# Ordering 24 in-projection matmuls behind the last filter's norm matmul, and giving the last job's rows of x buffers of their own

## The chip, the core and the metric

The kernel runs on one core of a Trainium2 chip. The metric is the device time of one execution in microseconds (us). TensorE (PE in the profile, with PEld for its weight loads) does the matrix products, VectorE (DVE) the elementwise work on two inputs, ScalarE (ACT) activations, casts and copies out of PSUM, GpSimd (POOL) some subtractions and some DMA issues, SyncE (SP) most DMA issues. Each engine works through its own instructions in the order in which the program lists them for that engine, and waits on semaphores for the others.

## The reference

An encoder layer is applied to two inputs of 1024 rows by 1024 channels, x_prompt (called x0 in the kernel) and x_sample (x1). Cut to what matters:

```python
p = rmsnorm(x, g_pre) @ w_in            # 8 sections of 1024 columns
fv, fg, hv, hg, mg = split(p)           # hv has 3 sections: v, x1, x2
y_f = (fft2_real(fv) * silu(fg)) @ w_fourier_out
v, x1, x2 = split(short_conv(hv, w_short))
z = v
for n, gate in enumerate((x1, x2)):
    z = gate * long_conv(z, kf[n], d[n])      # via FFT, with implicit filters
y_h = (z * silu(hg)) @ w_hyena_out
g_f, g_h = split(sigmoid(mg + b_merge))
return x + rmsnorm((g_f * y_f + g_h * y_h) @ w_out, g_post)
```

The filters `kf` (two orders n, 1024 channels) come from a small network, are multiplied by a decay, divided by the sum of their absolute values over all taps, and transformed. The last line adds the untouched rows of x to the normed output: those rows are the second thing that the change is about.

## The kernel before, in words

All large products are done in a split format: a number is stored as a high and a low part (`wh`, `wl`, `yh`, `yl` and so on), and each product is three matmuls (`mm3`, L469): high by high, high by low, low by high. So one in-projection tile (`inproj`, L838; 128 output channels by 1024 positions, PSUM tile `pin`) is 2 halves q of the contraction, by 2 halves n of the positions, by 4 blocks, by 3, that is 48 matmuls of 128x512, 24 for each q. The first q uses the first four blocks of x, the second q the other four. Two `pin` tiles fit in PSUM at once (`self.psum("mm", 2, "pin", L)`, L841). The weights of each q are loaded (`wr`), rounded on ACT (`wh`, L170) and the remainder is made on POOL (`wl`, L180), with three buffers for each.

The work goes through three phases. `phase_fourier` (L601) does the Fourier branch of both inputs. `phase_main` (L986) first makes the 16 filters in a loop over i (two orders n by eight channel tiles ct), then runs `branches` (L1039). `phase_tail` (L1169) does the remaining gates and the output products.

In the filter loop each filter has two parts. `filter_taps` (L736) makes the taps `T` and the sum of their absolute values in `acc`; its norm is two small products on PE into the tile `pn` (L765 and L766, recorded as two matmuls each), from which DVE makes the reciprocal `invn` (L767) and the skip term `db` (L768, L769). `filter_spectrum` (L773) forms even and odd parts on DVE (`fE`, `fO`, `xp`, `xm`), calls `butterfly` (L658: DVE and ACT make the pieces `b`, `bs`, `bh`, `bl`), then transforms each of four groups with `forward` (L704, tile `pXf`, L788) and turns the results on ACT (`ktmp`, L794, L803, L804) and DVE (`kt`). Between filters the loop runs gate tiles (`spill_gate`, L876), so that PE has in-projections to do. The loop is one filter ahead with its taps: the taps of the last filter are made before the spectrum of the last but one.

`branches` runs the steps of the long convolutions. Ahead of its loop stand `front(0)` (L1053: the in-projection and short convolution of the tile `v`, L1055, then transposes) and `gates(0)` (L1058: the in-projection of the first gate tile, here called x, by `conv(2, 0, ...)`). `conv` (L866) empties a `pin` tile with one activation on ACT (L871) and two operations on DVE (L872 and L873, recorded at L176), after which the PSUM is free. The output of `v` lies in a buffer tagged "u" that it shares with `xm` of the filter spectrum (L781, L869; one buffer); the output of x lies in a buffer tagged "x" (four buffers, shared with the taps). Step 1 then begins with another `v`, which needs a free `pin` tile.

What sets the order: the program is written for a tile framework that fixes each engine's order when the kernel is built. It steps through a simulated timeline and, whenever an engine is free in it, takes among the instructions whose inputs are there the one that stands first in the program. So a later in-projection slides in wherever PE would wait in that simulated timeline, ahead of instructions that stand before it in the program. `tc.issue_after(ins)` adds an order: what is traced in its block on the engine of `ins` is placed behind `ins`. No semaphore and no data dependence comes with it. On the chip each engine keeps the order that was fixed.

The end of the tail: the output product runs as eight jobs (`rows`, L1176), each two blocks of 128 rows. A job's first products are started one job ahead by `first` (L1245), which multiplies by the weight blocks `B11` and `B21`. `B11` lies in the cells x10 to x13 of the pool `xp` (L1431: `("B11", "x1{}", 60)`), and the eighth job's `first` is its last reader. `open_rows` (L1461) loads the job's rows of x (tile `xr`) on SP's queue into the cells st0 and st1 of the pool `gw`, one buffer each, so the load of one job follows the last read of the job before it. `half_row` (L1474) combines the products, `finish` (L1494) and, in the last job, `begin_norm` and `end_norm` (L1504, L1511) make the norm, and `close` (L1488) does `o = half * rs + x` (L1491, recorded at L176) and stores the result (tile `y`, L1492).

Of the kernel before, what the change touches and what calls it, by code (L numbers as in the profile page):

```python
# [16 lines left out]
P = 128  # L17
# [143 lines left out]
class K:  # L161
    def __init__(self, tc, a, dbg=None):
        self.tc, self.nc, self.a = tc, tc.nc, a
        self.dbg = dbg or {}


    def split(self, h, l, src, eng="pool", heng="act"):
# [568 lines left out]
    def filter_taps(self, n, ct, rates, ws):  # L736
        nc, a = self.nc, self.a
        w3, dec = rates
        w3s = ws.tile([P, 4, 256], F32R, tag="t1", name="w3s", bufs=1)
        w3h, w3l = w3s[:, 0], w3s[:, 1]  # L740
        self.split(w3h, w3l, w3, "dve", "act")
        T = [ws.tile([P, 2, 2, 2, P], F32, tag="x", name=f"T{i}", bufs=4) for i in range(2)]
        acc = ws.tile([P, 2, 2, P], F32, tag="yl", name="acc", bufs=2)
        accf = acc.rearrange("p a d c -> p (a d c)")
        for m in range(4):
            ps = self.psum("T", 2, "pft")
            ex = ws.tile([P, 512], F32, tag="yh", name="ex", bufs=2)
            for i in range(2):
                q = 2 * m + i
                s = slice(256 * i, 256 * i + 256)  # L750
                self.mm(ps[:, s], self.hid[:, q * P:(q + 1) * P], w3h, True, False)
                self.mm(ps[:, s], self.hid[:, q * P:(q + 1) * P], w3l, False, True)
                nc.scalar.activation(ex[:, s], dec, AF.Exp, scale=self.vec[:, q:q + 1])
            Tm = T[m // 2][:, m % 2].rearrange("p a d c -> p (a d c)")
            self.mul("dve", Tm, ps, ex)
            nc.scalar.activation(ex if m else accf, Tm, AF.Abs)
            if m:
                self.add("dve", accf, accf, ex)
        db = ws.tile([P, P], F32, tag="db", name="db", bufs=1)
        nc.sync.dma_start(db, a["hyena_d"][n, ct].partition_broadcast(P))  # L760
        self.add("dve", acc[:, 0], acc[:, 0], acc[:, 1])
        self.add("dve", acc[:, 0, 0], acc[:, 0, 0], acc[:, 0, 1])
        sm = acc[:, 0, 0]
        pn = self.psum("T", 2, "pn")
        nc.tensor.matmul(pn[:, 0:P], self.ones[:, 0:1].to_broadcast([P, P]), sm, start=True, stop=True)  # L765
        nc.tensor.matmul(pn[:, P:P + 2], sm, self.ones[:, 0:2], start=True, stop=True)  # L766
        nc.vector.reciprocal(self.invn[:, n * 8 + ct:n * 8 + ct + 1], pn[:, P:P + 1])  # L767
        self.mul("dve", db, pn[:, 0:P], db)  # L768
        self.stt("dve", T[0][:, 0, 1, 0], db, self.vec[:, 9:10], T[0][:, 0, 1, 0])  # L769
        nc.vector.tensor_scalar(T[1][:, 1, 0, 1], T[1][:, 1, 0, 1], self.vec[:, 8:9], None, op0=MUL)  # L770
        return T
# [66 lines left out]
    def inproj(self, sec, mt, b=None):  # L838

        nc, a = self.nc, self.a  # L840
        ps = self.psum("mm", 2, "pin", L)  # L841
        for q in range(2):
            s = slice(512 * q, 512 * q + 512)
            h = self.wp.tile([P, 4, P], F32R, tag="wh", name="wh", bufs=3)
            l = self.wp.tile([P, 4, P], F32R, tag="wl", name="wl", bufs=3)
            parts = [t.rearrange("p a b -> p (a b)") for t in (h, l)]
            kept = self.d_w[sec - 1][mt] if b is not None else None
            if b:
                for t, k in zip(parts, kept):
                    nc.sync.dma_start(t.bitcast(F32), k[:, s])  # L850
            else:
                r = self.wp.tile([P, 512], F32, tag="w", name="wr", bufs=2)
                nc.sync.dma_start(r, a["w_in"][sec, mt][:, s])
                self.split(*parts, r, "pool", "act")
                self.pooled = self.left
                if kept:
                    for t, k in zip(parts, kept):
                        nc.gpsimd.dma_start(k[:, s], t.bitcast(F32))
            for n in range(2):
                for kk in range(4):  # L860
                    k = 4 * q + kk
                    s = slice(512 * n, 512 * n + 512)
                    self.mm3(ps[:, s], (h[:, kk], l[:, kk]), self.X[k][n], k == 0, k == 7)
        return ps

    def conv(self, sec, ct, ws, name, b):  # L866
# [172 lines left out]
    def branches(self, nb, nct, ws, mi):  # L1039

        tc, nc = self.tc, self.nc
        steps = []
        for b in range(nb):
            steps.append((b, 0, 0))
            for c in range(1, nct):
                steps += [(b, 0, c), (b, 1, c - 1)]
            steps.append((b, 1, nct - 1))
        plain = list(self.PLAIN)  # L1050
        Z, X, G = {}, {}, {}

        def front(i):  # L1053
            b, n, c = steps[i]
            src = self.conv(1, c, ws, "v", b) if n == 0 else Z.pop(c)  # L1055
            return self.conv_front(src, ws)

        def gates(i):  # L1058
            b, n, c = steps[i]
            x = self.conv(2 + n, c, ws, f"x{n + 1}", b)  # L1060
            if n and b == 0:
                early = c < NH
                ps = None if early else self.inproj(4, c)
                sg = [self.wp.tile([P, 512], F32, tag="gt", name="sg", bufs=3) for q in range(2)]
                for q in range(2):
                    s = slice(512 * q, 512 * q + 512)
                    if early:
                        nc.sync.dma_start(sg[q], self.d_g[0][4][c][:, s])
                    else:
                        nc.scalar.activation(sg[q], ps[:, s], AF.Silu)  # L1070
                G[i] = sg, early
            X[i] = x

        def close(i):

            if i in G:
                sg, early = G.pop(i)
                for q in range(2):
                    s = slice(512 * q, 512 * q + 512)
                    if early:  # L1080
                        with tc.issue_after(self.rounded.ins):
                            nc.scalar.activation(sg[q], sg[q], AF.Silu)
                    self.mul("dve", X[i][:, s], X[i][:, s], sg[q])
        B = front(0)
        gates(0)
        for i, (b, n, c) in enumerate(steps):
            nxt = None
            if i + 1 < len(steps):
                nxt = front(i + 1)
                gates(i + 1)  # L1090
                if i + 2 < len(steps) and steps[i + 2][0] != steps[i + 1][0]:
                    self.load_x(steps[i + 2][0])
            y = self.conv_back(n, c, B, ws)
            close(i + 1)
            B = nxt
            for _ in range({4: 1, 3: 1, 2: 2, 1: 2}.get(len(steps) - i, 0)):
                self.spill_gate(b, *plain.pop(), ws)
            z = self.gate(n, c, y, X.pop(i))
            if self.due:
                mark = mi.tile([P, 1], F32R, tag="mark", name="mark", bufs=1)  # L1100
                with tc.issue_after(nc.gpsimd.tensor_copy(mark, z[:, 0:1]).ins):  # L1101
                    self.due.pop(0)()
            if n == 0:
                Z[c] = z
                continue
            nc.sync.dma_start(self.d_sh[b][c], z)
            if b == 0 and NF <= c:
                self.spill_gate(0, 0, c, ws)
        with tc.issue_after(self.ended.ins):
            for sec, c in plain:  # L1110
                self.spill_gate(1, sec, c, ws)
# [57 lines left out]
    def phase_tail(self):  # L1169
# [10 lines left out]
        with ExitStack() as es:  # L1180
# [277 lines left out]

            row = {}

            def open_rows(job):  # L1461
                u, t = job
                b, half = u // 2, u % 2
                where = [512 * half + P * (t + j) for j in range(2)]
                x, o = [], []
                for j in range(2):
                    x.append(flat(cell(gw, f"st{j}", "xr")))
                    nc.sync.dma_start(x[j], a[f"x{b}"][where[j]:where[j] + P, :])
                    o.append(flat(cell(xp, f"x0{4 + 2 * (t // 2) + j}", "o")))
                ss = op.tile([P, 2, 2], F32, tag="ss", name="ss", bufs=2)  # L1470
                row.update(b=b, at=where, x=x, o=o, ss=ss)
                return dict(row)
# [132 lines left out]
            Y["T4"] = quad(Z["T4"])  # L1605
            for i, job in enumerate(rows):
                final = i + 1 == len(rows)
                cur = open_rows(job)
                out = lambda job, j, n, p, q, op2: half_row(j, n, p, q, op2)
                pc, u = list(part2(out, job, A, Y, pa, pb, m1))[-1]  # L1610
                if i + 2 == len(rows):
# [105 lines left out]
```

## Time and profile before

| | us |
|---|---|
| median of three timed runs | 2370.41 (2368.41 to 2370.42) |
| the profiled execution, its own time | 2372.98 |
| span of its trace | 2371.2 |
| around the span | 1.78 |

The shares of the span by engine, with the work of the whole program: TensorE is busy for 2321.9 us of it, VectorE for 1970.2, ScalarE for 1118.7, GpSimd for 446.3. The mean clock that the throttle granted to TensorE is 0.996.

How to read it: a line of the timeline gives the start, the length, the engine, the line of the kernel, the operation, output and inputs and the number of instructions; where the engine stood idle before, the idle time and what ended it stand in square brackets. L193, L180, L176 and L170 are helpers that record most operations, so those go by the names of their tiles. A line of the table by windows gives, for a stretch of the trace, its length and the busy time of PE, PEld, DVE, ACT and POOL with the number of instructions, then the granted clock of TensorE, the mean share of the DMA engines and GB/s. Starts of instructions are used below for lengths of streams of matmuls, since these overlap.

### The profile page before, as it was taken

To read this page: it belongs to the slowest core of one execution; us is meant where nothing else is said; L and a number is where in the kernel's file an instruction comes from. 1 tells how busy PE (TensorE), PEld (TensorE's weight loads), DVE (VectorE), ACT (ScalarE), POOL (GpSimd) and SP (SyncE) were. 2 spreads that over 40 slices of the span, in tenths; PEclk is the share of its full clock that TensorE was granted. 3 is DMA by queue.
4 is the path that set the end of the run, shared out by engine and by line. 5 is a ranking of instruction groups with operands and counts; after the bars stand their busy time and mean duration, and the time that the engine had idled before them with its cause. 6 is when DMAs were issued, how large, how long until landed. Compare 5 with 4: busy or idle time off the path is not lost.

```text
span 2371.2 us, 36206 instructions
## 1 busy us (share of the span) xinstructions
PE 2321.9 (98%) x12784; PEld 2016.9 (85%) x12784; DVE 1970.2 (83%) x3438; ACT 1118.7 (47%) x2080; POOL 446.3 (19%) x428
## 2 busy tenths in 40 slices
PE   6999999999999999999999999999999999999998
PEld 5999888888878888888888888888888888888787
DVE  7775788887889999999889998997755578777987
ACT  6654676777653333334223232333443364566443
POOL 3342221222233342322000000122000000101311
PEclk9999999999999999999999999999999999999999
DMA  7636765555566666677464564445954678998654
GB/s 257 219 137 218 270 217 168 176 167 169 189 211 196 208 197 206 201 202 248 156 207 139 178 188 163 151 156 181 340 168 142 217 268 267 265 315 248 187 161 142
DMA packets 246207, 479.69 MB, mean 202 GB/s; under 512 B 24582, under 2 KB 82280, under 8 KB 245706
## 3 DMA queue, kind: packets, MB, share of 16 engines
q1 hardware_dynamic: 222013, 402.25, 51.0%
q0 software_dynamic: 23792, 75.11, 11.2%
q8 instruction: 100, 1.64, 0.3%
q14 instruction: 81, 0.66, 0.1%
q10 hardware_dynamic: 221, 0.04, 0.0%
HBM read 326.82 MB, written 177.73 MB: 213 GB/s over the span
## 4 chain that ended last, share of the span: by engine, by line
PE 54%; DVE 4%; issue 2%; DMA 1%; POOL 0%; ACT 0%; DVEq 0%; SPq 0%; POOLq 0%; ACTq 0%
PE pin L193 18%; PE pg L193 14%; PE pn L193 10%; PE pT L193 5%; PE pX L193 5%; PE tph L904 1%; DVE x L176 0%; DMA k<-d_k 0%; DMA d_m<-gt 0%; DVE t L180 0%; POOL d_m L1358 0%; DVE b L180 0%; DMA wl<-d_s 0%; DVE y L180 0%; DMA xr<-in_x 0%
## 5 line engine op out<-in xcount | busy, mean ns | idle before, releaser
L193 PE MATMUL pin<-x,wh 128*128 128x512 f32 x2816 | 889.7, 391 | 0.0
L193 PEld LDWEIGHTS pin<-x,wh 128*128 128x128 f32 x2816 | 524.4, 188 | 99.3
L193 PE MATMUL pin<-x,wl 128*128 128x512 f32 x1408 | 552.0, 392 | 0.0
L180 POOL TENSOR_TENSOR wl<-wr,wh 128x512 fp32r<-128x512 f32 x128 | 221.8, 1733 | 684.2 <-ACT wh L170 641.0
L193 PEld LDWEIGHTS pin<-x,wl 128*128 128x128 f32 x1408 | 265.2, 188 | 48.5
L193 PE MATMUL pn<-room,wh 128*128 128x512 f32 x864 | 266.4, 389 | 0.6 <-DVE gt L180 0.6
L193 PEld LDWEIGHTS pn<-room,wh 128*128 128x128 f32 x864 | 162.0, 188 | 35.0 <-issue 1.0
L193 PE MATMUL pn<-room,wl 128*128 128x512 f32 x432 | 168.4, 390 | 1.1 <-DVE wl L180 1.1
L180 DVE TENSOR_TENSOR t<-pX,k 128x1024 f32<-128x1024 f32 x128 | 155.7, 1217 | 9.0 <-PE pX L193 4.3
L193 PE MATMUL pX<-bh,cfwd 128*128 128x256 f32 x768 | 162.4, 288 | 0.0
L193 PE MATMUL pT<-cinv,yh 128*128 128x256 f32 x768 | 146.1, 285 | 3.6 <-DVE T0s L180 3.6
L170 ACT CAST wh<-wr 128x512 fp32r<-128x512 f32 x128 | 79.2, 619 | 135.5 <-PE pin L193 102.1
L170 ACT CAST bh<-b 128x512 fp32r<-128x512 f32 x144 | 88.5, 619 | 114.0 <-DVE b L180 82.2
L193 PEld LDWEIGHTS pT<-cinv,yh 128*128 128x128 f32 x768 | 123.0, 191 | 10.7 <-ACT T1s L957 2.7
L193 PEld LDWEIGHTS pX<-bh,cfwd 128*128 128x128 f32 x768 | 127.1, 190 | 2.8 <-issue 0.4
L1358 POOL DMA_DIRECT2D d_m<-gt x32 | 27.1, 848 | 534.0 <-DVE gt L180 497.8
L170 ACT CAST yh<-y 128x512 fp32r<-128x512 f32 x96 | 59.6, 620 | 124.2 <-DVE y L180 123.7
L193 PE MATMUL pT<-cinv,yl 128*128 128x256 f32 x384 | 109.3, 285 | 0.2 <-DVE yl L180 0.2
L193 PE MATMUL pX<-bl,cfwd 128*128 128x256 f32 x384 | 109.2, 284 | 0.0
L180 DVE TENSOR_TENSOR bl<-b,bh 128x512 fp32r<-128x512 f32 x144 | 102.3, 715 | 3.0 <-ACT bh L170 2.7
L1101 POOL CAST mark<-x 128x1 fp32r<-128x1 f32 x30 | 22.4, 746 | 412.3 <-DVE x L176 412.2
L180 DVE TENSOR_TENSOR y<-t 128x512 f32<-128x512 f32 x128 | 91.9, 718 | 6.5 <-PE pT L193 6.2
(362 smaller groups left out, 5174.0 us busy)
## 6 DMA issues: line engine op xcount, KB each, us to landing
k<-d_k SPq DMA_DIRECT2D x128, 512.0 KB, 4.3
wr<-in_w_in SPq DMA_DIRECT2D x128, 256.0 KB, 3.3
d_g<-gt SPq DMA_DIRECT2D x124, 256.0 KB, 3.0
wl<-d_s SPq DMA_DIRECT2D x56, 512.0 KB, 5.7
d_k<-kt SPq DMA_DIRECT2D x128, 128.0 KB, 2.4
d_k<-kt SPq DMA_DIRECT2D x64, 256.0 KB, 3.0
g<-d_g SPq DMA_DIRECT2D x64, 256.0 KB, 5.4
r<-d_g SPq DMA_DIRECT2D x60, 256.0 KB, 5.8
```

Of the source, the lines that this page charges most:

```text
L170: self.rounded = nc.scalar.copy(h, src)
L180: return e.tensor_tensor(out, a, b, op=op)
L193: return self.nc.tensor.matmul(out, lhsT, rhs, start=start, stop=stop, skip_group_check=shared)
L904: nc.tensor.transpose(tp[:, q * P:(q + 1) * P], eo[:, e, q], self.ident)
L1101: with tc.issue_after(nc.gpsimd.tensor_copy(mark, z[:, 0:1]).ins):
L1358: nc.gpsimd.dma_start(dst, t, accum_op=ADD)
```

## The change

It has two parts that share no code. The first: the norm matmul of L766 is remembered in `self.normed` (after the filter loop it is that of the last filter). While `gates(0)` is traced, `self.behind` holds it, and `inproj` puts the 24 matmuls of q = 1 into a block `issue_after`. The 24 of q = 0, the loads and the rounding of the weights, and all other calls of `inproj` are left as they are. The second: the last job of the output product loads its rows of x into the cells x10 and x11 of the pool `xp` instead of st0 and st1.

```diff
@@ filter_taps
-        nc.tensor.matmul(pn[:, P:P + 2], sm, self.ones[:, 0:2], start=True, stop=True)
+        self.normed = nc.tensor.matmul(pn[:, P:P + 2], sm, self.ones[:, 0:2], start=True, stop=True)
@@ inproj
-            for n in range(2):
-                for kk in range(4):
-                    k = 4 * q + kk
-                    s = slice(512 * n, 512 * n + 512)
-                    self.mm3(ps[:, s], (h[:, kk], l[:, kk]), self.X[k][n], k == 0, k == 7)
+            with self.tc.issue_after(self.behind.ins) if q and self.behind else ExitStack():
+                for n in range(2):
+                    for kk in range(4):
+                        k = 4 * q + kk
+                        s = slice(512 * n, 512 * n + 512)
+                        self.mm3(ps[:, s], (h[:, kk], l[:, kk]), self.X[k][n], k == 0, k == 7)
@@ branches
         B = front(0)
+        self.behind = self.normed
         gates(0)
+        self.behind = None
@@ open_rows
-            def open_rows(job):
+            def open_rows(job, own=False):
...
-                    x.append(flat(cell(gw, f"st{j}", "xr")))
+                    x.append(flat(cell(xp, f"x1{j}", "xr") if own else cell(gw, f"st{j}", "xr")))
@@ the loop over the jobs
-                cur = open_rows(job)
+                cur = open_rows(job, final)
```

`self.behind` is set to `None` in the constructor.

More of the change, by code (lines that the diff above doesn't have):

```diff
@@ L1084, in branches @@
         B = front(0)
+        self.behind = self.normed
         gates(0)
+        self.behind = None
         for i, (b, n, c) in enumerate(steps):
```

## The prediction

> **What bounds the kernel now.** I read the page first (who is busy, what ended last), then the chain of waits near the end, then what PE waits for, then the timeline at the two places that the change touches.
>
> ```profile
> PE 2321.9 (98%) x12784; PEld 2016.9 (85%) x12784; DVE 1970.2 (83%) x3438; ACT 1118.7 (47%) x2080; POOL 446.3 (19%) x428
> ...
> PE 54%; DVE 4%; issue 2%; DMA 1%; POOL 0%; ACT 0%; DVEq 0%; SPq 0%; POOLq 0%; ACTq 0%
> ```
>
> PE is hardly ever without work, and PE makes most of the chain that ended last. With the matmuls left as they are, time can only come from places where PE stands still, and from the tail behind its last matmul. The table by windows shows the one large hole of the main phase:
>
> ```profile
> 640.00:667.00 27.00, 27.00 (x151) 23.60 (x150) 24.01 (x58) 18.73 (x41) 10.17 (x12) 1.00 0.74 250
> 667.00:676.90 9.90, 9.90 (x57) 8.39 (x55) 6.67 (x18) 3.40 (x8) 2.33 (x3) 1.00 0.59 186
> 676.90:682.40 5.50, 0.00 (x0) 0.03 (x1) 5.50 (x14) 3.64 (x8) 2.69 (x3) 0.95 0.66 213
> 682.40:686.20 3.80, 3.80 (x21) 3.80 (x22) 3.80 (x8) 1.97 (x4) 0.00 (x0) 0.63 0.49 176
> ```
>
> PE does nothing for 5.50 us while DVE is busy for all of them, and the clock then stands at 0.63 for 3.80 us, which costs 3.80 x 0.37 = 1.4 us more. The timeline says who waits for whom:
>
> ```profile
> 671.12 0.38 PE L765 MATMUL pn<-acc,ones 128*128 128x128 f32 x2
> ...
> 671.48 0.48 PE L193 MATMUL pin<-x,wl 128*128 128x512 f32 x1
> 671.79 0.28 PE L193 MATMUL pXf<-bh,cfwd 128*128 128x256 f32 x1
> ...
> 674.67 0.63 PE L193 MATMUL pin<-x,wh 128*128 128x512 f32 x2
> ...
> 676.51 0.39 PE L193 MATMUL pin<-x,wl 128*128 128x512 f32 x1
> 682.40 1.19 PE L193 MATMUL pXf<-b,cfw 128*128 128x128 f32 x4 [5.50 <-DVE b L180]
> ...
> 686.12 0.63 PE L193 MATMUL pin<-x,wh 128*128 128x512 f32 x2
> ```
>
> The last filter's norm (pn, 671.12) is followed by the rest of the first gate tile's in-projection, and then by nothing until the butterfly of that filter gives b. The other end of that chain is on DVE:
>
> ```profile
> 666.43 0.28 DVE L180 TENSOR_TENSOR acc<-acc 128x128 f32<-128x128 f32 x1
> ...
> 669.14 0.61 DVE L176 SCALAR_TENSOR_TENSOR kt<-pXf,th,ktmp 128x128 f32<-128x128 f32 x2 [1.25 <-ACT ktmp L804]
> 671.65 0.17 DVE L767 RECIPROCAL invn<-pn 128x1 f32<-128x1 f32 x1 [1.91 <-PE pn L766]
> ...
> 680.65 1.27 DVE L176 SCALAR_TENSOR_TENSOR x<-pin,wsh,x 128x1023 f32<-128x1023 f32 x1
> 681.85 0.74 DVE L180 TENSOR_TENSOR b<-bs 128x256 f32<-128x256 f32 x2
> ...
> 684.46 1.27 DVE L176 SCALAR_TENSOR_TENSOR x<-pin,wsh,x 128x1023 f32<-128x1023 f32 x1
> ```
>
> acc, which pn sums up, is there at 666.43 + 0.28 = 666.71, yet pn runs 4.4 us later, and DVE loses 1.91 us waiting for it. From 671.65 on no line up to b at 681.85 carries a wait. So before b DVE is late because pn is late, and pn is late because in-projection matmuls stand ahead of it on PE.
>
> How many of the held 24 these are, the weights tell. Each half tile takes one of three weight buffers in turn (v's two, x's two, the next v's two), so the second half of the next v is cast when the 24 matmuls of x's first half are over (first line of these ACT rows):
>
> ```profile
> 667.96 0.62 ACT L170 CAST wh<-wr 128x512 fp32r<-128x512 f32 x1
> ...
> 677.60 1.09 ACT L871 ACTIVATE x<-pin,wsh 128x1024 f32<-128x1024 f32 x1
> ...
> 680.84 0.40 ACT L690 ACTIVATE bs<-bs 128x256 f32<-128x256 f32 x1
> ```
>
> From 667.96 to 671.12 are 3.16 us, 14 matmuls at 0.23 us (nine matmuls start from 674.67 to 676.51, eight steps of 0.23), and 10 come behind pn (one at 671.48, nine from 674.67). 14 + 10 are the 24 of q = 1: the count closes.
>
> The other place is the end of the program. Timeline of DVE, SP and ACT there:
>
> ```profile
> 2339.74 0.44 SPq L1468 DMA_DIRECT2D xr<-in_x  x1
> 2355.59 1.07 SPq L1492 DMA_DIRECT2D y<-o  x2
> 2356.76 0.41 SPq L1468 DMA_DIRECT2D xr<-in_x  x1
> ...
> 2358.23 0.43 SPq L1468 DMA_DIRECT2D xr<-in_x  x1
> ```
>
> ```profile
> 2362.50 0.16 DVE L1520 SCALAR_TENSOR_TENSOR ne<-ne 128x1 f32<-128x1 f32 x1
> 2363.61 0.29 ACT L1516 ACTIVATE ne<-ss,nb 128x1 f32<-128x1 f32 x1
> 2363.77 0.75 DVE L176 SCALAR_TENSOR_TENSOR o<-o,ne,xr 128x512 f32<-128x512 f32 x1 [1.11 <-DMA xr<-in_x]
> ```
>
> The last job's xr is issued only when the job before has read its own rows, its second block lands too late, and DVE waits 1.11 us for it with all else ready.
>
> **The change, part by part: the rows of x.** The loads move from 2356.76 and 2358.23 to the moment when cells x10 and x11 are free, that is when the last first product has read B11. The copy of that product and the later rows:
>
> ```profile
> 2341.62 0.57 ACT L1242 COPY m<-pg 128x512 f32<-128x512 f32 x1
> ...
> 2364.44 0.75 DVE L176 SCALAR_TENSOR_TENSOR o<-og,ne,xr 128x512 f32<-128x512 f32 x1
> ...
> 2365.10 0.68 DVE L180 TENSOR_TENSOR o<-pg,gp 128x512 f32<-128x512 f32 x1
> ```
>
> ```profile
> DMA to landing us min/median/max: 4.3/4.8/10.7
> ```
>
> So xr can go out by about 2341.6. On SP's queue it then stands behind the 2339.74 issue; the next thing behind it is the store at 2355.59, so a wait of 2 us there holds nobody up, and those stores lose the two issues of 0.4 us that stood among them. Even at the slowest landing of any xr in this trace (10.7 us, the tile's own view, last row above) it is there at 2353. The reader at 2363.77 then starts behind its own input at 2362.50 + 0.16 = 2362.66, and everything behind it on DVE moves up: 2364.44 to 2363.3, 2365.10 to 2364.0. What is late next is the scale that ACT makes at 2363.61 to 2363.90, needed only behind the operation of 2365.10, which would end near 2364.7. So the whole 1.1 us reach the last store. Bounds: 1.1 if nothing else is late, 0 if the stores' landing sets the end. I take **-1.1**.
>
> **The held matmuls.** No instruction is added or removed; 14 matmuls move from before pn to behind it, and no DMA moves with them, since loads and rounding stay outside the block. Behind pn on PE's queue nothing else could have run: both pin tiles are taken until x and v are emptied. Step by step:
>
> 1. pn can start when the 24 of q = 0 are done, at 667.96, and acc is there (666.71). It gains 3.16 us.
> 2. DVE's reciprocal stands behind kt, which ends at 669.14 + 0.61 = 669.75. So it moves from 671.65 to about 669.8: 1.9 us, the length of its wait, and not 3.16.
> 3. From there DVE has no gap, so b could come at 680.0 instead of 681.85. But the tile x still ends near 676.9 (PE has the same work up to there), so ACT empties it at 677.60 to 678.69 as before, and the butterfly's scales on ACT (last one 680.84 to 681.24), which stand behind that, gain less: with ACT working without pause behind 678.69 about 0.8 us.
> 4. So the hole ends 0.8 to 1.9 us sooner, and the next tile's matmuls (686.12) too: they need the PSUM of x, freed by the operation at 684.46, in the same DVE row of work.
>
> I take **-1.5** for this, nearer to DVE's own wait of 1.91, because the scales are the smaller part of what DVE does there. Ends of the range: -6.9 if the hole closes (5.50 + 1.4), and +1.7 where x is emptied later than now: if pXf (671.79), which needs the PSUM that kt reads, cannot start before 669.75, PE idles some 1.3 us behind pn, x ends that much later, and its two operations of 1.27 us may fall behind other DVE work: 2 x 1.27 less the 0.8 won.
>
> Does the gain last? Behind 700 PE and then DVE have no slack:
>
> ```profile
> 780.00:840.00 60.00, 60.00 (x366) 53.61 (x365) 59.71 (x97) 21.80 (x40) 21.86 (x22) 1.00 0.63 204
> ...
> 1020.00:1080.00 60.00, 60.00 (x357) 53.12 (x356) 60.00 (x95) 21.57 (x39) 17.52 (x21) 1.00 0.64 191
> ```
>
> ```profile
> 2240.12 109.15 PE pg L193 x480
> ```
>
> With PE full in both windows and in one piece of 109 us of the chain up to 2349, an earlier start is an earlier end, as long as the order behind it stays as it is.
>
> A rule weighed: the clock. After 5.50 us without work it was 0.63, and a shorter hole shows it too:
>
> ```profile
> 975.40 0.76 PE L193 MATMUL pT<-cinv,yh 128*128 128x256 f32 x2 [2.19 <-DVE T0s L180]
> ```
>
> ```profile
> 975.40:979.20 3.80, 3.80 (x14) 3.27 (x15) 3.80 (x7) 1.27 (x3) 0.00 (x0) 0.56 0.57 213
> ```
>
> ```profile
> 908.69 0.47 PE L193 MATMUL pT<-cinv,yh 128*128 128x256 f32 x2 [1.38 <-DVE T0s L180]
> ```
>
> ```profile
> 908.70:912.00 3.30, 3.23 (x21) 2.61 (x22) 3.30 (x6) 0.35 (x2) 0.99 (x2) 1.00 0.67 209
> ```
>
> A wait of 2.19 us left the clock at 0.56 for 3.80 us, one of 1.38 us left it at 1.00. A hole of 5.50 - 1.5 = 4.0 us should therefore still pay the 1.4 us, and I count no gain there. [...]
>
> **The sum** against the profiled execution: 2372.98 (span 2371.2 and 1.78 around it) - 1.1 - 1.5 = 2370.4. The median is 2.57 below that execution, so 2370.41 - 2.6 = **2367.8**, 0.11% less.
>
> **Rivals.**
> *Only the end gains.* The wait for pn goes, but emptying x (ACT at 677.60, DVE at 684.46) becomes the bound in its place and the next tile starts at 686.12 as now. For it: step 3 has only 0.8 us to spare. Against it: 1.91 us of DVE idle do vanish. 2370.4 - 1.1 = 2369.3.
> *The hole nearly closes and the clock stays.* If the fixed order also puts b ahead of the two operations on x (2 x 1.27 = 2.5 us of DVE), the hole shrinks by 1.9 + 2.5 = 4.4 to 1.1 us, below the 1.38 that left the clock alone. Then 4.4 + 1.4 + 1.1 = 6.9: 2363.5. Against it: x must be emptied anyway before 686.12, so part of it comes back.
> [...]
> *Slower: the order behind it is drawn anew.* The order of the whole main phase follows from a simulated timeline in which 14 matmuls now come later. In the stretch around 900 to 980 PE waits for DVE (T0s). If one operation of 1.27 us slides ahead of T0s at 908.69, the wait grows from 1.38 to 2.65, past the 2.19 that cost clock: 1.27 + 3.80 x 0.44 = 2.9 us. One such place cancels the gain (+0.3), two give 2373.6, three 2376.5; from three it is slower by over 0.2%. For it: DVE is at 59.71 and 60.00 of 60. Against it: if all engines shift alike, nothing changes places.
> *It doesn't do what it says.* The load of xr is placed late on SP for another reason, and the scheduler leaves pn where it is: 2370.4. Nothing in the rows asks for that.
>
> **How the numbers follow.** 0.2% is 4.74 us, about what a measurement of this kernel can tell from no change: faster is below 2365.7, slower above 2375.2. Forecast 0.47, of which 0.06 reach below 2365.7; only the end 0.18; hole nearly closed 0.11; clock kept at a longer hole 0.04, half of it below 2365.7; drawn anew 0.16, of which 0.09 lie above 2375.2; no effect 0.04. Faster 0.06 + 0.11 + 0.02 = 0.19; slower 0.09; same 0.72. The range is **2364.0 to 2372.5**: it takes in the forecast with both bounds of step 4 up to +1.7, only the end, and one further stall; it leaves out the better part of the closed hole (about 0.09) and the cases of two or three stalls (about 0.11).
>
> **What would show it.** The timeline around pn: it should start near 668, with 24 pin matmuls behind it instead of 10, the reciprocal near 669.8 without a wait on PE, and PE's hole near 4 us. At the end the o<-o,ne,xr row should carry no wait for DMA, with xr issued near 2342. Wrong would be: a wait of PE ahead of pn (acc later than the first half), a hole of 5 us still, a wait of ACT or DVE on pin that wasn't there, or new waits of PE on T0s between 900 and 980.

## The result and the profile after

The kernel after takes 2366.56 us (median of 22 runs, 2364.08 to 2370.73), the one before 2370.36 us (22 runs, 2368.07 to 2372.84). The ratio is 0.9986, with a 95% interval of 0.9980 to 0.9992: faster by 3.3 us (1.9 to 4.7), which is 0.14% and so within the 0.2% that the prediction calls the same. The profiled execution of after took 2366.49 us (span 2364.7), 6.5 less than that of before; the execution of before that was profiled lies 2.6 above its median, so the two traces exaggerate.

In all that follows helper lines are one or two higher than in before (L194, L181, L177, L171 are its L193, L180, L176, L170), and one execution may already be late against another with the same order: e3 (below) stands 2.6 us behind before ahead of the hole (the first matmul behind pn starts at 674.10 and 671.48). The same matmul ahead of pn (the last filter's first pft) starts at 658.25 in before and at 660.18 in after, so times near pn are compared less 1.93 us.

First the page, then the windows around the hole, in the columns of the table of before:

```profile
PE 2322.0 (98%) x12784; PEld 2019.3 (85%) x12784; DVE 1968.6 (83%) x3438; ACT 1117.0 (47%) x2080; POOL 449.8 (19%) x428
```

```profile
669.88:678.86 8.98, 8.98 (x53) 7.64 (x51) 8.41 (x19) 3.47 (x8) 2.34 (x3) 1.00 0.64 204
678.86:681.55 2.69, 0.00 (x1) 0.03 (x1) 2.69 (x8) 2.69 (x7) 1.69 (x2) 0.87 0.57 186
681.55:686.73 5.18, 4.61 (x21) 4.34 (x21) 5.18 (x11) 2.99 (x6) 0.61 (x2) 0.50 0.81 260
686.73:691.10 4.37, 4.37 (x10) 3.44 (x11) 4.37 (x8) 2.02 (x6) 0.00 (x0) 0.50 0.06 18
```

The single hole of 5.50 us is gone: PE idles 2.69 us and then 5.18 - 4.61 = 0.57 us. But the clock is at half for longer. It reads 0.50 without a break from 680.84 to 691.08 here and from 681.82 to 685.23 in before, and 1.00 ahead of that and behind it, so a window holds 2 x (1 - clock) x length of half clock: 0.70 + 5.18 + 4.37 = 10.2 us here, 0.55 + 2.81 = 3.4 us in the windows of before. At half clock the matmuls of 512 columns start 0.43 us apart (six steps from 687.72 to 690.28 in after), at full clock 0.23 (eight steps from 674.67 to 676.51 in before): nearly half of that time is lost, and half is reckoned below. The timelines of PE, DVE and ACT show the new order:

```profile
669.88 0.38 PE L766 MATMUL pn<-acc,ones 128*128 128x128 f32 x2
...
670.24 0.71 PE L194 MATMUL pin<-x,wh 128*128 128x512 f32 x2
...
676.63 0.63 PE L194 MATMUL pin<-x,wh 128*128 128x512 f32 x2
...
681.55 1.19 PE L194 MATMUL pXf<-b,cfw 128*128 128x128 f32 x4 [2.69 <-ACT bs L691]
```

```profile
669.48 0.34 DVE L177 SCALAR_TENSOR_TENSOR kt<-pXf,th,kt 128x128 f32<-128x128 f32 x1
670.41 0.17 DVE L768 RECIPROCAL invn<-pn 128x1 f32<-128x1 f32 x1 [0.60 <-PE pn L767]
...
671.96 0.60 DVE L177 SCALAR_TENSOR_TENSOR kt<-pXf,th,ktmp 128x128 f32<-128x128 f32 x2
...
680.52 1.22 DVE L181 TENSOR_TENSOR b<-bs 128x256 f32<-128x256 f32 x2
...
682.26 1.27 DVE L177 SCALAR_TENSOR_TENSOR x<-pin,wsh,x 128x1023 f32<-128x1023 f32 x1
...
685.31 1.27 DVE L177 SCALAR_TENSOR_TENSOR x<-pin,wsh,x 128x1023 f32<-128x1023 f32 x1
```

```profile
679.68 1.10 ACT L873 ACTIVATE x<-pin,wsh 128x1024 f32<-128x1024 f32 x1
...
681.09 0.40 ACT L691 ACTIVATE bs<-bs 128x256 f32<-128x256 f32 x1
```

pn stands ahead of all 24 matmuls of q = 1. Less the lateness it starts at 667.95, 3.17 us sooner than in before. The reciprocal no longer stands behind the pair of kt that ended at 669.75 in before: that pair now runs at 671.96, behind it. On DVE b now comes ahead of the first emptying of x (680.52 and 682.26; in before 681.85 and 680.65). So pXf starts at 679.62, less the lateness, 2.8 us sooner, and then a second, small gap opens: PE waits for the second emptying of x, which ends at 685.31 + 1.27 = 686.58 (684.65 less the lateness, 685.73 in before).

At the end of the program, DVE and SP:

```profile
2357.02 0.16 DVE L1524 SCALAR_TENSOR_TENSOR ne<-ne 128x1 f32<-128x1 f32 x1
2357.27 0.75 DVE L177 SCALAR_TENSOR_TENSOR o<-o,ne,xr 128x512 f32<-128x512 f32 x1
```

```profile
2334.26 1.99 SPq L1472 DMA_DIRECT2D xr<-in_x  x3
2350.11 11.62 SPq L1496 DMA_DIRECT2D y<-o  x8
```

The last rows of x are issued by 2336.3 and the wait of 1.11 us on their DMA is gone.

Last, the stretch at 900 to 980 us, which the change doesn't touch. The list of PE's waits from 880 to 1000, before and then after (us in total, times, longest):

```profile
PE pT L193 <- DVE T0s L180: 3.6, 2, 2.2
PE pT L193 <- DVE yl L180: 0.2, 1, 0.2
```

```profile
PE pT L194 <- DVE T0s L181: 0.5, 1, 0.5
PE pX L194 <- DVE b L181: 0.5, 1, 0.5
```

And the order has changed there. The two traces list PE's matmuls in the same order up to pn; from there to the end of the main phase the order differs on all five engines (a comparison line by line gives 1928 lines of difference among PE's 12784 matmuls, 778 on DVE). The held matmuls alone do this (e1 below); the rows of x alone (e2) change only the places of their two loads in SP's list, at the end.

### The profile page after: what moved, and what is told of

It reads as the page before. It is cut to its first block, busy times and chain, and to the rows that moved or that the text cites. A ratio compares the mean times of both kernels' runs of the same rounds, so it can differ in the third digit from the quotient of the medians.

```text
span 2364.7 us, 36212 instructions
## 1 busy us (share of the span) xinstructions
PE 2322.0 (98%) x12784; PEld 2019.3 (85%) x12784; DVE 1968.6 (83%) x3438; ACT 1117.0 (47%) x2080; POOL 449.8 (19%) x428
## 4 chain that ended last, share of the span: by engine, by line
PE 55%; DVE 2%; DMA 1%; ACT 1%; issue 1%; POOL 0%; DVEq 0%; POOLq 0%; ACTq 0%; SPq 0%
PE pin L194 18%; PE pg L194 15%; PE pn L194 12%; PE pT L194 5%; PE pX L194 5%; PE tph L906 1%; DMA x<-d_x 1%; DMA xr<-in_x 0%; DMA d_m<-gt 0%; DMA k<-d_k 0%; DVE x L177 0%; DVE wl L181 0%; DVE t L181 0%; DVE wraw L181 0%; ACT room L171 0%
## 5 line engine op out<-in xcount | busy, mean ns | idle before, releaser
L194 PE MATMUL pin<-x,wh 128*128 128x512 f32 x2816 | 891.5, 392 | 0.6 <-DVE x L177 0.6
L194 PEld LDWEIGHTS pin<-x,wh 128*128 128x128 f32 x2816 | 525.3, 189 | 100.7 <-ACT v L873 0.8
L194 PE MATMUL pin<-x,wl 128*128 128x512 f32 x1408 | 552.1, 392 | 0.0
L181 POOL TENSOR_TENSOR wl<-wr,wh 128x512 fp32r<-128x512 f32 x128 | 224.6, 1755 | 709.7 <-ACT wh L171 682.0
L194 PEld LDWEIGHTS pin<-x,wl 128*128 128x128 f32 x1408 | 265.6, 189 | 50.0
L194 PE MATMUL pn<-room,wh 128*128 128x512 f32 x864 | 266.1, 389 | 0.0
L194 PEld LDWEIGHTS pn<-room,wh 128*128 128x128 f32 x864 | 162.1, 188 | 33.6 <-DVE gt L181 0.2
L194 PE MATMUL pn<-room,wl 128*128 128x512 f32 x432 | 168.4, 390 | 0.1
L181 DVE TENSOR_TENSOR t<-pX,k 128x1024 f32<-128x1024 f32 x128 | 156.2, 1220 | 8.7 <-PE pX L194 7.4
L194 PE MATMUL pX<-bh,cfwd 128*128 128x256 f32 x768 | 161.3, 288 | 0.0
L194 PE MATMUL pT<-cinv,yh 128*128 128x256 f32 x768 | 145.4, 284 | 0.5 <-DVE T0s L181 0.5
L171 ACT CAST wh<-wr 128x512 fp32r<-128x512 f32 x128 | 79.3, 619 | 132.7 <-PE pin L194 96.5
L171 ACT CAST bh<-b 128x512 fp32r<-128x512 f32 x144 | 88.7, 620 | 96.2 <-DVE b L181 65.5
L194 PEld LDWEIGHTS pT<-cinv,yh 128*128 128x128 f32 x768 | 122.8, 191 | 6.5 <-issue 0.6
L194 PEld LDWEIGHTS pX<-bh,cfwd 128*128 128x128 f32 x768 | 126.3, 190 | 2.2
L171 ACT CAST yh<-y 128x512 fp32r<-128x512 f32 x96 | 59.4, 619 | 117.7 <-DVE y L181 117.7
L194 PE MATMUL pX<-bl,cfwd 128*128 128x256 f32 x384 | 109.2, 284 | 0.0
L194 PE MATMUL pT<-cinv,yl 128*128 128x256 f32 x384 | 108.9, 284 | 0.0
L181 DVE TENSOR_TENSOR bl<-b,bh 128x512 fp32r<-128x512 f32 x144 | 101.5, 709 | 3.4 <-ACT bh L171 3.3
L907 ACT COPY xt<-tph 128x512 f32<-128x512 f32 x64 | 36.9, 587 | 128.7 <-PE tph L906 128.6
```

Source lines behind the costliest of these rows:

```text
L171: self.rounded = nc.scalar.copy(h, src)
L181: return e.tensor_tensor(out, a, b, op=op)
L194: return self.nc.tensor.matmul(out, lhsT, rhs, start=start, stop=stop, skip_group_check=shared)
L907: nc.scalar.copy(xt[:, e].rearrange("p a b -> p (a b)"), tp)
```

## The experiments

**The theories.** Theory 1: the local gain of the prediction's step 4, 1.5 us at the hole, is carried to the end. Theory 2: next to nothing is won at the hole; the gain comes from the order that is drawn anew further down. Theories 2a, 2b and 3 came up on the way and are told where they did.

Every time is against runs of before taken beside it on the same chip (7 to 11 runs of each kernel, 12 to 33 of before). Differences in the text are worked out from the ratio:

| | what is run | median us | before, beside it | ratio (95%) |
|---|---|---|---|---|
| e1 | held matmuls alone | 2367.33 | 2369.37 | 0.9988 (0.9979 to 0.9997) |
| e2 | rows of x alone | 2368.74 | 2369.37 | 0.9999 (0.9990 to 1.0008) |
| e3 | before again | 2369.49 | 2369.37 | 0.9996 (0.9987 to 1.0005) |
| e4 | after again | 2367.44 | 2369.37 | 0.9989 (0.9980 to 0.9998) |
| e5 | after's order near the hole only | 2367.57 | 2370.17 | 0.9993 (0.9984 to 1.0002) |
| e6 | after's order further down only | 2368.46 | 2370.17 | 0.9996 (0.9987 to 1.0005) |
| e7 | after's order at 840 to 1045 us only | 2369.41 | 2370.17 | 0.9994 (0.9986 to 1.0003) |
| e8 | e6 and the rows of x | 2368.49 | 2370.17 | 0.9992 (0.9983 to 1.0000) |
| e9 | before, gate loads later | 2369.05 | 2369.68 | 0.9992 (0.9983 to 1.0001) |
| e10 | after, gate loads later | 2365.32 | 2369.68 | 0.9980 (0.9972 to 0.9989) |
| e11 | after, x emptied earlier | 2364.25 | 2369.68 | 0.9976 (0.9965 to 0.9986) |
| e12 | after, both moves | 2362.88 | 2369.42 | 0.9974 (0.9964 to 0.9985) |

An interval is about 4 us wide and the parts in question are 1 to 3 us, so the times alone seldom decide. The traces do better, because the matmuls kept a steady pace (at full clock those of 128x512 start 0.23 us apart in before, and the second row is 0.00 in all six executions of before's order): the table gives, for stretches between the starts of the N-th of the 12784 matmul records, how much longer (+) or shorter (-) each execution took than the first profile of before. An execution stands on the left where it has before's order in that stretch, on the right where it has after's.

| matmuls (us) | before's order | after's order |
|---|---|---|
| 3800 to 4060 (650 to 702) | before 0, e2 +1.50, e3 +0.47, e6 +0.11, e7 +1.45, e8 +0.38, e9 +0.42: mean +0.62 | after +0.78, e1 +0.35, e4 +0.37, e5 +0.34, e10 -1.23: mean +0.12 |
| 4060 to 4800 (702 to 827) | 0.00 in all six | +0.72 in all eight |
| 4800 to 6000 (827 to 1035) | before 0, e2 -2.02, e3 -5.01, e5 -5.50: mean -3.13 | after -6.60, e1 -5.55, e4 -5.57, e6 -5.31, e8 -5.20, e11 -5.64: mean -5.65 |
| 6000 to 10800 (to 1907) | -0.19 to +0.05 | -0.40 to +0.32 |
| 10800 to 12783 (to 2363) | 0 to -2.03: mean -1.38 | +0.32 to -2.39: mean -1.58 |

Two things have to be known to read it. e7 stands in neither column of its third row, since it has after's order for the most of that stretch only (-5.83). And the N-th matmul is not the same matmul in both orders. Counted by shape, after's order has 7 more matmuls of 512 columns and 7 fewer of 256 among the 740 of the second row, and 5 and 2 the other way round in the next two rows. In before's trace the former start 0.23 us apart and the latter 0.12, so 7 of them are worth about 0.8 us, and PE never waits in the second row in either order: the +0.72 is work done earlier, not time lost. From 4060 to 10800 both have done the same work. There before's order (before, e2, e3, e5) stands at -3.1 in the mean and after's order (after, e1, e4, e6, e8, e11) at -5.0, so the order behind the hole is worth 1.9 us by these traces, not the 2.5 of the third row.

**e1, the held matmuls alone**: after, with `open_rows(job, False)`.

> The held matmuls alone; the last job's rows of x are loaded as before. Theory 1 (the local gain of the prediction's step 4): 1.0 to 1.9 us under before, of it 1.5 at the start of the next tile's matmuls, about 15 us behind pn, and nothing added later. Theory 2 (the gain comes from the order that is drawn anew further down): 1.5 to 3.5 us under before, with pn about 3.1 earlier than in before at equal lateness ahead of it, but the gain used up within 25 us by a half clock that lasts over three windows of 3.41 us instead of one, and 3 to 6 us gained between 900 and 1045 us where two waits on T0s go.

Measured: 2.8 us under before (0.7 to 5.0). At the hole it stands at +0.35, where Theory 1 wants -1.5; at 827 to 1035 it gains. The list of PE's waits at 655 to 705 tells why the hole gives nothing:

```profile
PE pXf L194 <- ACT bs L691: 2.7, 1, 2.7
PE pin L194 <- ACT bh L171: 2.6, 1, 2.6
```

5.3 us in two pieces, where before has 5.5 in one. They are the two pieces of e4 (below), which stands at +0.37 in the first row with a half clock of 3.4 us, not the 10.2 of after. So the gain at the hole is used up without the long half clock too, that part of Theory 2 was wrong, and the size of the gain further down rests on the first profile of before, an unlucky one (below).

**e2, the rows of x alone**: after without the two assignments to `self.behind`.

> The rows of x alone; the matmuls keep the order of before. Both theories: 0.7 to 1.1 us under before, all of it in the last 20 us: o<-o,ne,xr without a wait on a DMA. The start of the N-th matmul differs from before by no more than the jitter of the start, and by the same amount everywhere behind 700 us.

Measured: 0.2 us under before (2.4 under to 1.9 over), which excludes neither 0 nor 1.1. The trace decides: from the start of the last pair pg<-oB,s4h to the end of the span are 9.19, 9.28 and 9.24 us with the old loads (before, e3, e1) and 8.16, 8.16 and 8.18 with the new (e2, e4, after). So 1.07 us. The wait of `o<-o,ne,xr` on the DMA is 1.1 to 1.5 us in all seven executions with the old loads (e5, e6, e7 and e9 are the others) and gone in all seven with the new. The second half of the expectation failed: with before's order unchanged, PE's lateness did not stay the same behind 700 us.

**e3, before again** (a copy whose lines are numbered as in after) and **e4, after again.**

> Before's instructions and order, its lines numbered as in after. Both theories: within 0.05% of before (1.2 us). Its profile tells which of the waits at 900 to 980 us and 2190 to 2240 us belong to the order (Theory 2: the waits on T0s and the half clock behind 975 us come again) and which to one execution (Theory 1: they don't).

> After once more, on the same chip as the others. Both theories: 3.0 to 4.5 us under before. Theory 1: sum of the held matmuls' 1.5 and the rows' 1.1, so about 2.6 to 3; Theory 2: the sum of e1's and e2's differences, and the half clock behind the hole near 680 us lasts three windows again.

e3 is 0.9 us under before and so within its 1.2. e4 is 2.6 under (0.5 to 4.7), short of its 3.0 to 4.5, though the 3.3 of the first measurement lies within its interval. e3's trace lacks most of what the first profile of before had at 900 to 980 (3.6 us of waits for T0s and, from 975.37, half clock for 3.41): PE waits 1.0 us in all for T0s, and it is 5.0 us quicker from 827 to 1035 with the very same order. So the 6.6 us that the two first traces differ by there are for the greater part one execution's bad luck, and only what before's order does on average, 2.5 us in that row or 1.9 for equal work, can be the order's. With values from 0 to -5.5 on the left that mean is uncertain by more than 1 us. PE's idle time from 827 to 1035 us says the same: 3.9, 3.4, 1.0 and 1.7 us in before, e2, e3 and e5, 0.9 to 1.5 us in the six of after's order. Two of the four in before's order are level with after's. In e4 the half clock lasts 3.4 us (3.94 x 0.43 x 2 in the last row below) and not 10.2, so what Theory 2 expected of it did not come:

```profile
678.39:681.08 2.69, 0.00 (x1) 0.03 (x1) 2.69 (x8) 2.69 (x7) 1.70 (x2) 1.00 0.57 186
681.08:683.64 2.56, 2.56 (x20) 2.35 (x20) 2.56 (x5) 0.87 (x3) 0.61 (x2) 1.00 0.98 270
683.64:686.26 2.62, 0.00 (x1) 0.03 (x1) 2.62 (x7) 2.16 (x4) 0.00 (x0) 1.00 0.64 249
686.26:690.20 3.94, 3.94 (x10) 3.08 (x11) 3.94 (x8) 1.73 (x5) 0.00 (x0) 0.57 0.00 0
```

Here one sees where the local gain goes. pXf runs at full clock and is done in 2.56 us (3.72 in before, 682.40 to 686.12, of which 2.83 are at half clock), then PE idles again until x is emptied, and the half clock falls on the in-projections. They start 1.3 us earlier than in before (686.26 less 1.46 of lateness, against 686.12), and about 3.94 x 0.43 = 1.7 us of clock (an estimate) are lost on them at once. In before the half clock lay over pXf. With the 2.56 us of e4, pXf would have been done there at 684.96 (an estimate), and the next matmuls would have waited until x was emptied at 685.73 anyway. The same holds for e3 and e9: pXf takes 4.17 and 4.16 us (from 685.02 and 685.03) and would with 2.56 have been done at 687.6, ahead of the emptying of x at 688.35 and 688.36; the in-projections behind it run at full clock (0.23 us apart). e7 waits 5.5 us at the hole as before does and yet stands at +1.45 in the first row, with e2 beside it at +1.50: an estimate from these numbers is that in both the half clock reached into the in-projections.

**e5 to e8: the order of one part with that of the other.** In these kernels each engine's order is written out from lists taken from the built programs of before and after (without its rows of x, except in e8), by an order-only edge from each instruction to the next:

```diff
+    for order in ORDER:
+        for i, j in zip(order, order[1:]):
+            tc.add_manual_dep(ins[j], ins[i].name, NoSync, reason="in_order")
```

> Every engine's order fixed: that of after (without its rows of x) up to the next tile's tph, about 702 us, and that of before from there. Theory 1 (a gain at the hole that is carried to the end): 1.0 to 1.9 us under before. Theory 2 (nothing is won near the hole, the gain lies in the order further down): within 0.7 us of before; the waits of the matmuls on T0s at 900 to 980 us come again, 1.0 to 3.6 us in all, and the stretch from the 4800th to the 6000th matmul is no shorter than in executions of before's order (0 to 5.0 us under the first one).

> The other half: before's order up to the next tile's tph, so pn stands behind the 14 matmuls again, and the order of after (without its rows of x) from there. Theory 1: as before, within 0.7 us. Theory 2: 1.5 to 3.5 us under before with a hole of 5.5 us left as it is; waits on T0s at 900 to 980 us of 0.5 us or less.

> Before's order everywhere except between the matmuls that start at about 840 and 1045 us, which with the other engines' work beside them stand in the order of after. Theory 1: within 0.7 us of before. Theory 2: 2.0 to 4.0 us under before, since the 0.7 us that the order of after loses between 702 and 827 us is left out too; waits on T0s of 0.5 us or less and no half clock in 900 to 1045 us.

> e6 with the rows of x in buffers of their own: the change without its held matmuls, with the order that they led to. Theory 1: 1.0 under before, from the end alone. Theory 2: 2.6 to 4.5 under before, so as fast as after or faster, though pn stands as late as in before.

By their times all four are unclear (1.7, 0.9, 1.4 and 1.9 us under before, each with about 2 us to either side); e6 misses the 1.5 to 3.5 of Theory 2, e7 its 2.0 to 4.0 and e8 its 2.6 to 4.5, and e5 would fit Theory 1 (that e7 leaves out 0.7 us of loss was a wrong reason, as said under the table). By the traces one half of Theory 2 holds: e5 has pn early and two gaps of 2.7 and 2.6, and stands at +0.34 behind them, in the middle of the executions of before. The other half is not shown: e6, e7 and e8 keep the hole of 5.5 and gain 5.2 to 5.8 on the first profile at 827 to 1035, but e3 and e5 gain 5.0 and 5.5 there with before's order. In e5 T0s is waited for again, in e7, whose order differs from before's in that stretch alone, less (PE's waits, 880 to 1000, e5 then e7):

```profile
PE pT L194 <- DVE T0s L181: 1.7, 1, 1.7
```

```profile
PE pT L194 <- DVE T0s L181: 0.5, 1, 0.5
PE pX L194 <- DVE b L181: 0.5, 1, 0.5
```

But e5's stretch was as quick as those of after's order (-5.50), so the stall is no fixed price of before's order. What decides it in one execution? DVE's row ahead of the first stall, in before and in e5:

```profile
897.05 1.23 DVE L180 TENSOR_TENSOR t<-pX,k 128x1024 f32<-128x1024 f32 x1 [2.43 <-DMA k<-d_k]
```

```profile
896.11 1.23 DVE L181 TENSOR_TENSOR t<-pX,k 128x1024 f32<-128x1024 f32 x1 [1.40 <-DMA k<-d_k]
```

DVE itself waits, for a filter spectrum k. The DMA view of that place (880 to 905, after) shows the company in which k travels:

```profile
k<-d_k SPq DMA_DIRECT2D x3, 512.0 KB, 8.1
d_s<-in_w_fo POOLq DMA_DIRECT2D x1, 1024.0 KB, 13.3
...
sg<-d_g SPq DMA_DIRECT2D x2, 256.0 KB, 6.8
```

Over the whole run the median landing of k is 4.3 us in before and 4.2 in after; here it is 8.1 (6.0 in before), beside 1 MB of d_s and, shortly ahead of it on the same queue, two gate loads sg of 256 KB. The gate loaded at 885 isn't read by ACT before 943.

**e9 and e10: the gate loads later.** Theory 2a: the stall is a load's, k landing late behind sg. Theory 2b: DVE has too much to do there. The edit to SP's list, for e9 in before's order, for e10 in after's:

```diff
-sg<-d_g x2
 k<-d_k
 k<-d_k
 k<-d_k
 k<-d_k
+sg<-d_g x2
```

> Before's order on every engine, but each pair of gate loads sg<-d_g stands behind the next four issues of k<-d_k on SP instead of ahead of them. Theory 2a (the stall at 890 to 980 us is a load's: k lands late behind the 512 KB of sg, DVE waits for it, PE then for T0s): DVE's waits at t<-pX,k at 897 and 957 us fall from 1.3 to 2.4 and 0.9 to 1.4 us to under 0.5 each, the stretch from the 4800th to the 6000th matmul is 4 to 6.5 us under that of the first profile of before, the time 1 to 3 us under before. Theory 2b (the stall is the order's own: DVE has too much to do there): the waits on T0s stay, time within 0.7 us of before.

> The same edit on after. Theory 2a: DVE's wait of 3.8 to 4.4 us on k at 898 us falls by 2 us or more; PE hardly waits there in after (0.5 us on T0s), so the time is 0 to 1 us under after, 3 to 4.5 us under before. Theory 2b: no change of the waits.

DVE's only wait for k there, in e9 and in e10 (3.3 to 5.0 us in the seven executions with after's order there, e7 among them, without the edit; for after and for e3's 1.3 the label names PE, but k landed 0.1 us ahead of DVE's start, as in the others):

```profile
898.68 1.23 DVE L181 TENSOR_TENSOR t<-pX,k 128x1024 f32<-128x1024 f32 x1 [0.42 <-DMA k<-d_k]
```

```profile
896.15 1.23 DVE L181 TENSOR_TENSOR t<-pX,k 128x1024 f32<-128x1024 f32 x1 [2.35 <-DMA k<-d_k]
```

So in after's order sg holds k up, as 2a has it: the wait is 0.9 us or more shorter, though 2 us were expected, and, with each trace's lateness at 702 us taken off, DVE starts on k at 895.1 in e10, at 896.0 to 897.7 in the seven. In before's order the wait falls from 1.3 to 2.4 us to 0.42 (none came at 957, as none did in e3), but there it is less clear: DVE also came to that row 0.6 us later than in before, e2 and e3, and its start on k (895.6) lies within the range without the edit (893.8 to 897.1). The stretch from 827 to 1035 stands at -5.23 in e9, no better than e3's -5.01, and -7.42 in e10, better than any of after's order. The time of e9 is 1.9 us under before (4.0 under to 0.2 over), not proven. That PE still waits 1.0 us for T0s in e9, exactly as in e3, shows that the load is not the whole stall; the 1 MB of d_s beside it was not tried. e10 is 4.7 us under before (2.6 to 6.6), a little past its 3.0 to 4.5, but in its profile 1.7 of it are at the hole (-1.23 against +0.46 in the other four on the right), where the half clock happened to lie over pXf.

**e11: x emptied earlier.** Theory 3: what the earlier pn won is lost because the next tile's matmuls wait until x is emptied. One instruction of DVE moved, all else after's order:

```diff
 x<-pin,wsh,x
+x<-pin,wsh,x
 b<-bs,xm x2
 b<-xm,bs x2
 kt<-pXf,th,ktmp x2
-x<-pin,wsh,x
```

> After's order, with one instruction of DVE moved: the second x<-pin,wsh,x behind the hole stands right behind the first, ahead of two pairs of b and one of kt. Theory 3 (what the earlier pn won is lost because the next tile's matmuls wait until this instruction has emptied their buffer): the second gap in PE falls from 2.6 us (or 0.6 us with a half clock in front) to under 0.8 us, and PE stands 1.2 to 2 us earlier from there on, 2.5 to 3.5 if no half clock follows the shorter gaps. Rival (ACT's cast of bh ends last, as the wait's label says): the gap stays.

```profile
680.78 0.97 PE L194 MATMUL pXf<-b,cfw 128*128 128x128 f32 x4 [2.69 <-ACT bs L691]
...
684.74 0.62 PE L194 MATMUL pin<-x,wh 128*128 128x512 f32 x2
```

```profile
681.50 2.59 DVE L177 SCALAR_TENSOR_TENSOR x<-pin,wsh,x 128x1023 f32<-128x1023 f32 x2
```

The second gap is gone. PE stands at -2.55 at 702 us, 2.7 us earlier than the mean of after's order, more than the 1.2 to 2 expected with a half clock, though one of 3.4 us did follow (0.57 over 3.96 us): it lay over pXf, which took 3.96 us for 2.56, and since x was emptied only at 684.09 no more than 684.74 - 684.09 = 0.65 us of that were lost (an estimate). The rival (ACT's bh, as the wait's label said) falls. The time is 5.7 us under before (3.3 to 8.3), 2.3 to 3.2 us under after's two medians; the intervals of the ratios still touch.

**e12: both moves.**

> After's order with both moves of e10 and e11: the gate loads behind four issues of k, the second emptying of x behind the first. By Theory 2a and Theory 3 the gains are at different places (677 to 690 us; 880 to 990 us) and add: PE 2.5 to 3 us earlier behind the hole than in the first profile of before, DVE's wait on k at 898 us about 2.3 us instead of 3.8 to 4.4, the time 5 to 7 us under before. By the rival, that e10 was faster only because its one profile and runs met a shorter half clock at the hole: the time of e11, 5.0 to 5.7 under before.

Measured: 6.2 us under before (3.6 to 8.5), the fastest kernel of the study, though not distinguishable from e11 by its interval. Its trace shows both gains: -2.95 at the hole, -7.38 at 827 to 1035, DVE's wait for k 2.5 us. And it shows the hole without any half clock:

```profile
677.60:680.31 2.71, 0.03 (x2) 0.03 (x1) 2.71 (x8) 2.70 (x7) 1.69 (x2) 1.00 0.56 184
680.31:683.76 3.45, 2.56 (x21) 2.39 (x21) 3.42 (x5) 0.87 (x3) 0.61 (x2) 1.00 1.01 311
```

## Why the prediction was right, and where its reasons were not

The time came as forecast. One of the two terms was right for its reason. The other came near in size in good part by luck: its local gain was taken back by the clock, and by the traces most of what was measured came from places to which the prediction gave nothing.

- **Rows of x, -1.1**: right. 1.07 us by three executions against three, the wait on DMA gone, xr issued 14 us ahead of the first of the eight stores.
- **Held matmuls, -1.5**: e1 measured -2.8 (-0.7 to -5.0), but by the traces not from where the prediction took it. The stretches sum up to -0.5 at the hole (with +1.5 to -1.2 as the executions' spread) and -1.9 from 702 to 1907: -2.4. With the rows -3.4, beside the measured -3.3. The times of e5 to e8 are too wide to confirm this split.
- *Step 1* (pn 3.16 sooner, 24 matmuls behind it): right. (That nothing else could have run behind pn overlooks pXf at 671.79, in the prediction's own rows; nothing rests on it.)
- *Step 2* (the reciprocal only 1.9 sooner, behind kt) failed: it kept before's order on DVE. The order was drawn anew right there, kt fell behind, and the reciprocal came as early as pn, 3.2 us sooner, with a wait of 0.60 us for it.
- *Step 3* (the hole ends 0.8 to 1.9 sooner): it ended 2.8 us sooner, since on DVE b now stood ahead of the emptying of x.
- *Step 4* (the next tile's matmuls earlier by the same): their start moved by 1.3 us in after, e1, e4 and e5, within the 0.8 to 1.9, but for another reason, and not by the 2.8 of pXf. The bound was the emptying of x, as the rival "only the end gains" had it, though that rival let the start stay where it was; e11 shows the bound by taking it away. The rival "the hole nearly closes" had named both halves of this: b ahead of the two operations on x, and that part of the gain comes back because x must be emptied anyway.
- *The clock* ("I count no gain there") was the step that failed in size. The clock was held to cost 1.4 us in either case. In before it lay over pXf, behind which PE would have had to wait anyway; in e4 it lay over in-projections (0.57 from 686.26 to 690.20) and took the 1.3 us back (e1 and e5, with the same two gaps, end alike: +0.35 and +0.34 beside +0.37). In after it even lasted 10.2 us. In e10 it lay over pXf again (0.62 from 680.50 to 684.50), and there the hole gave -1.23.
- *"As long as the order behind it stays as it is"*: it did not. The rival "drawn anew" came, in the stretch that was named, but, as far as the traces tell, with the opposite sign: PE waits less there on average in the new order. That it could go either way was missed. Both orders wait for the load of k there, in after's order for longer on DVE (3.3 to 5.0 us against 1.3 to 2.4), and yet PE stalls less. Why the new order is less sensitive to that load stays open, and four executions against six do not make the 1.9 us certain.

The 0.04 for a clock kept at a longer hole, half of which is in the 0.19 for faster, is a figure that no run shows. What the runs showed: gaps of about 2.7 us kept the full clock in e12 and at the first of e4, and the same 2.69 us in after, e10 and e11 were followed by half clock (last section).

## What to carry to other kernels

Where a framework draws the order from a simulated timeline, one edge moves everything behind it: compare the two built orders before you put a gain down to the edit, and fix the rest of the order when you want to know what the edit itself does. A hole ends only when the last of its releasers comes: after mending the first, look for the next operation that frees the buffer (here two operations of 1.27 us on DVE, one of which stood three places too late). And take several profiles of one kernel before you explain a stretch; with the same order this one gave values 5.5 us apart.

## What the runs showed of the hardware

Whether a gap of PE was followed by half clock did not go by its length alone:

| execution | PE idle, us | clock at its end and behind it |
|---|---|---|
| before | 5.50 (to 682.40) | 0.50 for 3.41 us, from 681.82 |
| before | 2.19 (to 975.40) | 0.50 for 3.41 us, from 975.37 |
| before | 1.38 (to 908.69) | 1.00 |
| after | 2.69 (to 681.55), then 0.57 (to 686.73) | 0.50 for 10.24 us, from 680.84 |
| e4 | 2.69 (to 681.08) | 1.00 |
| e4 | 2.62 (to 686.26) | 0.57 over 3.94 us, so half for 3.4 |
| e10 | 2.69 (to 681.94) | 0.62 from 680.50 to 684.50, 0.96 to 689.00, so half for 3.4 |
| e11 | 2.69 (to 680.78) | 0.57 over 3.96 us, so half for 3.4 |
| e12 | 2.68 (in 677.60 to 680.31), then 0.89 (in the next 3.45 us) | 1.00 |

Gaps of 2.7 us thus ended in all three ways: no half clock in e12 and at the first of e4, 3.4 us of it in e10 and e11, 10.2 us in after. What decides between them was not shown.

A second point: the 512 KB load of k lands in 4.3 us in the median of before and 4.2 in that of after, and in after took 8.1 us (median of the three from 880 to 905) where two gate loads of 256 KB stood ahead of it on the same queue and 1 MB was on its way on another. With the gate loads behind it (e10) it took 5.0, and DVE got it 1.0 to 2.6 us sooner.
